# Lower weight halves from a negating ScalarE copy and an adding DMA

## Chip, core and metric

The kernel runs on one core of a Trainium2 chip. The core has TensorE (PE: matrix multiplications, and PEld: the loads of their stationary operand), VectorE (DVE), ScalarE (ACT), GpSimd (POOL) and SyncE (SP), which issues DMAs. Each engine works through its own queue in order; semaphores order work between engines. 16 DMA engines move data between DRAM, the on-chip memory SBUF, and back. TensorE writes its sums into eight banks of PSUM. The metric is the device time of one execution in microseconds (us), as the median of several runs.

## The reference

The reference is one inference step of a decoder with two layers and a width of 1024, for 512 prompt tokens and 64 sample tokens (8 sequences of 8) that share all weights. The first layer mixes tokens by a pooling mixer, the second by a gated delta-rule mixer (GDN) with a short convolution and a recurrent state; after each mixer stands a SwiGLU feed-forward block (FFN) of width 2816. All is float32. Most of the work is in products with weights:

```python
def swiglu(h, w_in, w_out):
    gu = h @ w_in
    return (jax.nn.silu(gu[..., :D_FF]) * gu[..., D_FF:]) @ w_out
...
    # gdn_mixer
    proj = h @ w_in
    qkv = proj[..., :GDN_CONV_DIM]
    z = proj[..., GDN_CONV_DIM:GDN_CONV_DIM + GDN_V_DIM]
...
    y = o.reshape(B, L, GDN_V_DIM).astype(h.dtype) @ w_out
```

Between these stand norms, the convolution, the chunked delta rule (triangular solves, a scan over chunks of 64 tokens) and the gate. Returned are the outputs of both groups and their new pooling, convolution and recurrent states.

## The kernel before

**Products in three passes.** The products are made in the format float32r (F32R in the code), to which a copy of a float32 tile is rounded. Each float32 operand w is kept as two F32R tiles: the upper half h = round(w) and the lower half l = w - h. A product is the sum of three matrix products, wh by ah, wh by al and wl by ah, all into one PSUM bank. The function `mm3` (lines 663 to 669) writes them in turn for each of up to 8 blocks of 128 rows, so the first product with wl comes right after the first two with wh:

```python
            PE.matmul(ps, wh[:, k], ah, start=first and k == 0, stop=False)
            PE.matmul(ps, wh[:, k], al, start=False, stop=False)
            PE.matmul(ps, wl[:, k], ah, start=False, stop=last and k == nk - 1)
```

**Weight tiles.** A weight tile is 1024 rows by 128 columns (896 rows in 48 of the loads of `ffn_w_out`), laid out as 128 partitions by 8 blocks by 128 columns: 512 KB, which in DRAM are 1024 runs of 512 bytes. `Weights.load` (line 650) takes a buffer `wraw`, lets SyncE issue the DMA, and calls `split` (line 655): ScalarE copies `wraw` into `wh`, which rounds; then VectorE subtracts, `wl = wraw - wh`. The subtraction may go to GpSimd instead (`EITHER`), where the planner finds that better. `wraw`, `wh` and `wl` have three buffers each (`Weights(ctx, 3, 3)`, line 838); a buffer can be filled again when the instructions that use its earlier content are done. There are 257 calls of `load` (one of them for a tile of only 32 columns); two more tiles, those of the pooling mixer (`load_pw`, line 923), call `split` directly after their own DMAs.

**Token halves.** The 576 tokens are worked on as two halves of 256 and 320 tokens (`HALVES`), which use PSUM banks "A" and "B". In the FFN (`ffn`, line 759) the weights are walked in 68 chunks: gate and up columns of a block of 7 or 8 slices of the hidden width, then the eight output columns of that block. In the middle of the walk one loaded tile serves both halves. At the beginning (14 chunks in the first layer, 10 in the second) and at the end (the last 8 chunks) the first half runs through all these chunks, and then the second half, and each half loads the weights anew:

```python
            for half in range(2):
                for i in range(lo, hi):
                    run(i, half, load(i))
```

The GDN output projection does the same for its second 1024 rows (line 1707). The GDN input projections, in four groups of heads, use each tile for both halves and lie between the delta-rule work of the groups.

**Order of the work.** The kernel doesn't issue its instructions as it writes them. The class `Plan` records them with their dependencies (data, and reuse of buffers) and simulates the five engines with a cost for each instruction (`cost`, line 143): how long it holds its engine and when its result is there. `forward` (line 339) places instructions on engines by priority; `finish` (line 250) repeats that with changed priorities 40 times and issues the best order found, engine by engine. For a DMA the model holds SyncE 60 ns, and lets transfers follow one another at 240 bytes per ns (`forward`, lines 468 to 470). In the model VectorE and GpSimd exclude each other for some instructions (lines 460 to 465). Where TensorE would be idle the planner puts matrix products of no use (`ps_w`). Nearly every instruction is thus issued from one line of `finish`, line 283, so profile rows are told apart by tile names.

Of the kernel before, what the change touches and what calls it, by code (L numbers as in the profile page):

```python
# [12 lines left out]
F32R = mybir.dt.float32r  # L13
I32 = mybir.dt.int32
AF = mybir.ActivationFunctionType
ALU = mybir.AluOpType
# [4 lines left out]
P = 128  # L21
# [29 lines left out]
class Plan:  # L51
# [91 lines left out]
    def cost(self, eng, method, out, ins, k):  # L143

        n = self.size(out)
        if method == "dma_start":
            return 60.0, 2000.0 + n * list(out.ap)[0][1] * 4 / 240.0
        ps = any(x.space == PSUM for x in ins)
        if eng == "PE":
            rows = self.rows(ins[0])  # L150
            if ins[0].dtype != F32:
                t = 0.4375 * n + 6.5
            elif method == "transpose":
                t = max(n / 1.2 + 2, 62.0)
            else:
                t = 2 * (n / 1.2 + 4.5)
                if rows == 128:
                    t = max(t, 220.0) if "tile_position" not in k else max(t / min(3.2, 128 / list(out.ap)[0][1]), 80.0)
                elif k.get("tile_position"):
                    t = t * 0.55 if rows == 64 else 62.0  # L160
            return t, t + 165
        if eng == "ACT":
            extra = 93 * sum(self.is_ap(k.get(w)) for w in ("scale", "bias")) + (100 if "accum_out" in k else 0)
            t = 0.833 * max(n, 16) + (170 if ps else 205) + extra
            return t - 102, t
        if eng == "POOL":
            if method in ("memset", "tensor_copy"):
                t = 0.85 * n + (100 if method == "memset" else 183)
            elif method == "affine_select":
                t = 1.1 * n + 190  # L170
            else:
                bc = any(list(x.ap)[-1][0] == 0 for x in ins if self.size(x) > 1)
                t = (1.75 if bc else 2.2) * n + 180
            return t - 60, t
        if method == "transpose":
            flat = all(list(x.ap)[-1][0] == 1 for x in ins + [out])
            t = 1.27 * n + 50 if flat else 1.95 * n + 80
        elif method == "scalar_tensor_tensor":
            t = 1.04 * n + 210
        elif method == "reciprocal":  # L180
            t = 6.2 * n + 153
        elif method in ("tensor_copy", "tensor_scalar") and not ps:
            t = 0.58 * n + 160
        else:
            t = 1.04 * n + 160
        return t - 85, t
# [152 lines left out]
    def forward(self, rank):  # L339
        ops, succ = self.ops, self.succ  # L340
        n = len(ops)
# [5 lines left out]
        mode, dma = {}, 0.0  # L347
# [10 lines left out]
        def note(t, work):  # L358
            nonlocal busy, fast
            for p in phases:  # L360
                while int((t + p[0]) / self.WINDOW) > p[3]:
                    p[1:] = 0.0, 1.0 if p[1] >= self.LOAD * self.WINDOW else 2.0, p[3] + 1
                p[1] += work
            fast = sum(p[2] for p in phases) / 4
            busy += work
            recent.append((t, work))
            while recent and recent[0][0] <= t - self.WINDOW:
                busy -= recent.popleft()[1]
# [36 lines left out]
        while todo:  # L405
            best = None
            for e in free:
                q, r = avail[e], ready[e]
                while q and taken[q[0][1]]:
                    heapq.heappop(q)  # L410
                while r and taken[r[0][1]]:
                    heapq.heappop(r)
                if q:
                    t = free[e]
                elif r:
                    t = max(free[e], r[0][0])
                else:
                    continue
                if best is None or t < best[0]:
                    best = t, e  # L420
            t, e = best
            if e == "PE" and t > free[e] + 300.0:
                idle_until(t)
            while ready[e] and ready[e][0][0] <= t:
                _, i = heapq.heappop(ready[e])
                if not taken[i]:
                    heapq.heappush(avail[e], (-rank[i], i))
            q = mine = avail[e]
            if e == "POOL":

                spare = sum(ops[y[1]][1]["DVE"][0] for y in avail["DVE"] if not ops[y[1]][8] and not taken[y[1]])
                spare += max(free["DVE"] - max(t, port["DVE"]), 0.0)
                mine = [x for x in q if not taken[x[1]] and ("DVE" not in ops[x[1]][0] or
                        spare > self.SPARE * ops[x[1]][1][e][0])]
                if not mine:
                    soon = [r[0][0] for r in (ready[e], ready["DVE"]) if r and r[0][0] > t]
                    if free["DVE"] > t:
                        soon.append(free["DVE"])
                    free[e] = max(t + 50.0, min(soon, default=t))
                    continue  # L440
            elif e == "DVE" and port["POOL"] > t + 300:
                mine = [x for x in q if not taken[x[1]] and not ops[x[1]][8]] or q
            i = self.take(e, mine, taken, mode.get(e))
            if mine is not q:
                q.remove((-rank[i], i))
                heapq.heapify(q)
            hold, done = ops[i][1][e]
            m = ops[i][5]
            if m and m != mode.get(e):
                if e in mode:  # L450
                    change = self.TURN[e][abs(m - mode[e]) > 500]
                    hold, done = hold + change, done + change
                mode[e] = m
            if e == "PE":
                note(t, ops[i][6])
                done += hold * (fast - 1)
                hold *= fast
            taken[i] = True
            todo -= 1
            if e == "DVE" and ops[i][8] or e == "POOL" and ops[i][9] != "memset":  # L460
                other = port["POOL" if e == "DVE" else "DVE"]
                late = max(other - 130.0 - t, 0.0)
                hold, done = hold + late, done + late
                if e == "DVE" or ops[i][9] == "tensor_tensor":
                    port[e] = t + done
            free[e] = t + hold
            end = t + done
            if e == "SP":
                dma = max(dma, t + 1400) + (done - 2000)
                end = dma + 600  # L470
            order.append((i, e))
            times.append((t, end))
            for name in ops[i][10]:
                still[name] -= 1
                quiet[name] = max(quiet.get(name, 0.0), end)
            for j in succ[i]:
                at = t + hold if ops[j][7] == e == "PE" else end + self.LAT[ops[j][7]]
                when[j] = max(when[j], at)
                left[j] -= 1
                if not left[j]:  # L480
                    arrive(j)
# [17 lines left out]
def hybrid_kernel(  # L499
# [11 lines left out]
    PE, ACT, DVE, POOL, SP = (plan.engine(**{name: real}) for name, real in (  # L511
        ("PE", nc.tensor), ("ACT", nc.scalar), ("DVE", nc.vector), ("POOL", nc.gpsimd), ("SP", nc.sync)))
# [68 lines left out]
    nk = sp.tile([P, SP1, KH], F32, name="nk")  # L581
# [63 lines left out]
    class Weights:  # L645
# [3 lines left out]

        def load(self, src, row, col, nk, n=P, eng=EITHER):  # L650
            raw = self.p.tile([P, 8, P], F32, name="wraw", tag="wraw", bufs=self.raw)[:, :nk, :n]
            SP.dma_start(raw, src[row:row + nk * P, col:col + n].rearrange("(k p) m -> p k m", p=P))
            return self.split(raw, eng)

        def split(self, raw, eng=EITHER):
            _, nk, n = raw.shape
            h = self.p.tile([P, 8, P], F32R, name="wh", tag="wh", bufs=self.bufs)[:, :nk, :n]
            l = self.p.tile([P, 8, P], F32R, name="wl", tag="wl", bufs=self.bufs)[:, :nk, :n]
            ACT.activation(h, raw, AF.Copy)
            eng.tensor_tensor(l, raw, h.bitcast(F32), op=sub)  # L660
            return h, l
# [177 lines left out]
    with ExitStack() as s0:  # L839
        xp = pool("xp0", stack=s0)  # L840
        x = xp.tile([P, NC, T], F32, name="x")
        y = {o0: xp.tile([P, NC, n], F32, name="y%d" % o0) for o0, n in HALVES}
        tp = pool("tp0", stack=s0)
        with ExitStack() as st:
# [12 lines left out]
            for g0, src in ((G_MPRE, norm_mix_pre), (G_MPOST, norm_mix_post), (G_FPRE, norm_ffn_pre),  # L857
                            (G_FPOST, norm_ffn_post), (G_PS, pool_scale)):
                n = src.shape[0] * NC
# [72 lines left out]
            for hi, (o0, n) in enumerate(HALVES):  # L932
                tag = "AB"[hi]
# [25 lines left out]
                for gi, g in enumerate((3, 2, 1, 0)):  # L959
# [20 lines left out]
                    wh, wl = pw[g // 2 * 2]  # L980
# [716 lines left out]
    x = xp.tile([P, NC, T], F32, name="x1")  # L1697
# [105 lines left out]
```

## Time and profile before

| | |
|---|---|
| time, median of 2 runs | 1650.04 us (1646.67 to 1653.41) |
| span of the profiled execution | 1654.1 us (the page gives no time outside the span) |
| busy TensorE (PE) | 1620.4 us, 98% |
| busy VectorE / ScalarE / GpSimd | 1002.7 / 699.4 / 119.5 us |
| mean granted TensorE clock | 0.989 |
| DMA | 185.25 MB, mean 112 GB/s |
| read from DRAM, written to it | 157.73 MB, 25.77 MB |

How to read it: a row names the line, the engine, the operation, the tile written and, after the arrow, the tiles read. Groups end with the busy time, the mean of one instruction in ns, and the idle time of the engine just before them with what ended most of it. `ps_A`, `ps_B`, `ps_m` and the like are PSUM banks, so rows of PE go by the bank and the operands. PE's matmuls are pipelined: one row of 309 ns overlaps the next. The chain of waits is followed back from the last instruction. In the table by stretches each engine has its busy time and, in brackets, the count of its instructions; then follow the granted clock (1.00 is full), the mean busy share of the 16 DMA engines and what they moved. The DMA engines' share can come out a little above 1 in a window of one microsecond.

### The profile page before, as it was taken

How to read it: one execution, taken by the hardware profiler on the slowest of the kernel's cores; microseconds unless marked ns; L12 is line 12 of the kernel's file. 1: busy time of each engine (PE TensorE's matmuls, PEld its weight loads, DVE VectorE, ACT ScalarE, POOL GpSimd, SP SyncE). 2: the span in 40 equal slices, each digit the busy share in tenths (PEclk: the TensorE clock that was granted, in tenths of full speed). 3: DMA queues.
4: the chain of work that ended last, by engine and by line, in shares of the span. 5: the costliest groups of instructions: out<-in, count | busy, mean ns of one | idle time of the engine just before them, and what ended most of it. 6: DMA issues, size and time to landing. Idle time of an engine off the chain costs nothing. (4 is left out here: it accounts for less than half of the span.)

```text
span 1654.1 us, 30525 instructions
## 1 busy us (share of the span) xinstructions
PE 1620.4 (98%) x12317; PEld 1567.2 (95%) x12317; DVE 1002.7 (61%) x2074; ACT 699.4 (42%) x1434; POOL 119.5 (7%) x265
## 2 busy tenths in 40 slices
PE   8999999999999999999999999999999999999997
PEld 8999999999999998998898899899999999999997
DVE  6784223333387798997998899656694312233244
ACT  6653233212365944553453554424464322222244
POOL 3010000000001010021121131100000000000000
PEclk8899999999999999999999999999999999999999
DMA  6255322223366233324323423557544323223333
GB/s 175 67 157 146 90 77 81 86 77 90 92 171 167 84 104 93 100 75 137 89 77 104 116 78 116 163 167 244 171 135 135 102 75 92 72 79 92 87 102 113
DMA packets 329812, 185.25 MB, mean 112 GB/s; under 512 B 12235, under 2 KB 324140, under 8 KB 329407
## 3 DMA queue, kind: packets, MB, share of 16 engines
q1 hardware_dynamic: 329671, 183.30, 38.2%
q8 instruction: 97, 1.59, 0.4%
q14 instruction: 44, 0.36, 0.1%
HBM read 157.73 MB, written 25.77 MB: 111 GB/s over the span
## 5 line engine op out<-in xcount | busy, mean ns | idle before, releaser
L283 DVE TENSOR_TENSOR wl<-wraw,wh 128x1024 fp32r<-128x1024 f32 (+2 forms) x253 | 301.9, 1201 | 292.1 <-PE ps_A L283 102.6
L283 ACT ACTIVATE wh<-wraw 128x1024 fp32r<-128x1024 f32 (+2 forms) x259 | 266.4, 1035 | 481.5 <-PE ps_A L283 185.9
L283 PE MATMUL ps_m<-hH,wh 128*128 128x256 f32 (+1 forms) x832 | 239.1, 309 | 1.4 <-ACT zz L283 1.2
L283 PE MATMUL ps_m<-hL,wh 128*128 128x256 f32 (+1 forms) x832 | 238.9, 308 | 0.0
L283 PE MATMUL ps_m<-hH,wl 128*128 128x320 f32 (+1 forms) x832 | 236.7, 309 | 0.0
L283 PE MATMUL ps_B<-hL,wh 128*128 128x320 f32 x768 | 224.2, 311 | 0.3 <-DVE hL L283 0.3
L283 PE MATMUL ps_B<-hH,wl 128*128 128x320 f32 x768 | 223.9, 311 | 0.1
L283 PE MATMUL ps_B<-hH,wh 128*128 128x320 f32 x768 | 223.3, 311 | 0.3 <-ACT sg L283 0.3
L283 PE MATMUL ps_A<-hH,wh 128*128 128x256 f32 x768 | 205.6, 285 | 1.3 <-DVE yo L283 1.3
L283 PE MATMUL ps_A<-hL,wh 128*128 128x256 f32 x768 | 204.1, 284 | 0.0
L283 PE MATMUL ps_A<-hH,wl 128*128 128x256 f32 x768 | 202.7, 284 | 0.1
L283 PEld LDWEIGHTS ps_m<-hH,wh 128*128 128x128 f32 x832 | 152.5, 190 | 6.5 <-ACT zz L283 1.8
L283 PEld LDWEIGHTS ps_m<-hL,wh 128*128 128x128 f32 x832 | 152.5, 190 | 2.2 <-DVE hL L283 0.2
L283 PEld LDWEIGHTS ps_m<-hH,wl 128*128 128x128 f32 x832 | 151.8, 190 | 2.8 <-issue 0.9
L283 PEld LDWEIGHTS ps_A<-hH,wh 128*128 128x128 f32 x768 | 142.8, 191 | 2.3 <-issue 1.4
L283 PEld LDWEIGHTS ps_A<-hL,wh 128*128 128x128 f32 x768 | 142.7, 191 | 0.2
L283 PEld LDWEIGHTS ps_A<-hH,wl 128*128 128x128 f32 x768 | 141.8, 191 | 0.4 <-DVE wl L283 0.2
L283 PEld LDWEIGHTS ps_B<-hL,wh 128*128 128x128 f32 x768 | 141.2, 189 | 0.6 <-DVE hL L283 0.5
L283 PEld LDWEIGHTS ps_B<-hH,wl 128*128 128x128 f32 x768 | 141.2, 189 | 0.5 <-DVE wl L283 0.2
L283 PEld LDWEIGHTS ps_B<-hH,wh 128*128 128x128 f32 x768 | 140.4, 189 | 0.9 <-ACT sg L283 0.5
L283 PE MATMUL ps_B<-aH,wh 128*128 128x320 f32 x352 | 102.1, 311 | 0.0
L283 PE MATMUL ps_B<-aL,wh 128*128 128x320 f32 x352 | 102.0, 310 | 0.0
(388 smaller groups left out, 3109.1 us busy)
## 6 DMA issues: line engine op xcount, KB each, us to landing
wraw<-in_ffn_w_in_dram SPq DMA_DIRECT2D x112, 512.0 KB
wraw<-in_gdn_w_in_dram SPq DMA_DIRECT2D x56, 512.0 KB
wraw<-in_ffn_w_out_dram SPq DMA_DIRECT2D x48, 448.0 KB
wraw<-in_gdn_w_out_dram SPq DMA_DIRECT2D x24, 512.0 KB
wraw<-in_ffn_w_out_dram SPq DMA_DIRECT2D x16, 512.0 KB
St<-in_state_gdn_rec_dram SPq DMA_DIRECT2D x32, 256.0 KB
out_dram<-St SPq DMA_DIRECT2D x32, 256.0 KB
z_d<-zz SPq DMA_DIRECT2D x16, 288.0 KB
```

The source lines that it names most:

```text
L283: calls[e](*a, **k)
```

## The change

`Weights.load` no longer calls `split`. After the load of `wraw` ScalarE first writes the negated upper half into the tile of the lower half, `l = -round(wraw)` (a copy with scale -1.0 into an F32R tile). GpSimd then issues a DMA that reads the same weights from DRAM a second time and adds them to that tile, `l += w`. Last ScalarE writes `h = round(wraw)` as before. `wl` now depends on ScalarE and on two DMAs, and no longer on VectorE or on `wh`. The two pooling tiles keep `split`. The planner's model is told of the new instruction: a DMA issued from GpSimd holds that engine 1000 ns, takes twice the transfer time of one from SyncE in the common DMA stream, and is left out of the exclusion between VectorE and GpSimd.

```diff
         if method == "dma_start":
-            return 60.0, 2000.0 + n * list(out.ap)[0][1] * 4 / 240.0
+            return 60.0 if eng == "SP" else 1000.0, 2000.0 + n * list(out.ap)[0][1] * 4 / 240.0
...
-            if e == "DVE" and ops[i][8] or e == "POOL" and ops[i][9] != "memset":
+            if e == "DVE" and ops[i][8] or e == "POOL" and ops[i][9] not in ("memset", "dma_start"):
...
-            if e == "SP":
-                dma = max(dma, t + 1400) + (done - 2000)
+            if ops[i][9] == "dma_start":
+                dma = max(dma, t + 1400) + (done - 2000) * (1 if e == "SP" else 2)
                 end = dma + 600
...
         def load(self, src, row, col, nk, n=P, eng=EITHER):
             raw = self.p.tile([P, 8, P], F32, name="wraw", tag="wraw", bufs=self.raw)[:, :nk, :n]
-            SP.dma_start(raw, src[row:row + nk * P, col:col + n].rearrange("(k p) m -> p k m", p=P))
-            return self.split(raw, eng)
+            w = src[row:row + nk * P, col:col + n].rearrange("(k p) m -> p k m", p=P)
+            SP.dma_start(raw, w)
+            h, l = self.tiles(nk, n)
+            ACT.activation(l, raw, AF.Copy, scale=-1.0)
+            POOL.dma_start(l, w, accum_op=ALU.add)
+            ACT.activation(h, raw, AF.Copy)
+            return h, l
+
+        def tiles(self, nk, n):
+            return tuple(self.p.tile([P, 8, P], F32R, name=x, tag=x, bufs=self.bufs)[:, :nk, :n] for x in ("wh", "wl"))
 
         def split(self, raw, eng=EITHER):
             _, nk, n = raw.shape
-            h = self.p.tile([P, 8, P], F32R, name="wh", tag="wh", bufs=self.bufs)[:, :nk, :n]
-            l = self.p.tile([P, 8, P], F32R, name="wl", tag="wl", bufs=self.bufs)[:, :nk, :n]
+            h, l = self.tiles(nk, n)
             ACT.activation(h, raw, AF.Copy)
             eng.tensor_tensor(l, raw, h.bitcast(F32), op=sub)
             return h, l
```

## Prediction

> **What bounds the kernel now.** I read the page from the top: the span, the busy table, the chain of waits by line, the costliest groups.
>
> ```profile
> span 1654.1 us, 30525 instructions
> ...
> PE 1620.4 (98%) x12317; PEld 1567.2 (95%) x12317; DVE 1002.7 (61%) x2074; ACT 699.4 (42%) x1434; POOL 119.5 (7%) x265
> ...
> PE ps_B L283 16%; PE ps_A L283 13%; PE ps_m L283 4%; PE ps_s L283 1%; PE ps_k L283 1%; PE ps_n L283 1%; DVE ac L283 1%; DMA yo<-y_d 0%; PE ps_w L279 0%; PE ps_x L283 0%; DVE wl L283 0%; DVE ii L283 0%; ACT wh L283 0%; DVE xT L283 0%; DMA og<-og_d 0%
> ...
> L283 DVE TENSOR_TENSOR wl<-wraw,wh 128x1024 fp32r<-128x1024 f32 (+2 forms) x253 | 301.9, 1201 | 292.1 <-PE ps_A L283 102.6
> L283 ACT ACTIVATE wh<-wraw 128x1024 fp32r<-128x1024 f32 (+2 forms) x259 | 266.4, 1035 | 481.5 <-PE ps_A L283 185.9
> ```
>
> TensorE is busy 98% of the span and idle for 1654.1 - 1620.4 = 33.7 us. The subtraction that the change removes costs VectorE 301.9 us, but in the chain of waits "DVE wl" has 0%. So VectorE is relieved where nothing waits for it, and the most that any relief can give is those 33.7 us, 2.0% of the span. A measurement of this kernel can tell about 2% (33 us) from no change.
>
> The average hides two kinds of stretches, so I read the busy table by stretches. The first table is of the whole kernel; the second, of the same stretches, is of the instructions that touch wl alone. There DVE (x) plus POOL (x) counts the weight tiles that are split.
>
> ```profile
> core 0: us, PE busy (x) PEld busy (x) DVE busy (x) ACT busy (x) POOL busy (x), PEclk, DMA share, GB/s
> 59.00:108.00 49.00, 49.00 (x383) 48.32 (x383) 40.21 (x89) 27.99 (x50) 4.41 (x5) 0.95 0.48 139
> 108.00:155.00 47.00, 46.67 (x315) 46.09 (x316) 25.54 (x38) 20.62 (x32) 0.00 (x0) 1.00 0.48 140
> 155.00:430.00 275.00, 275.00 (x2067) 274.92 (x2066) 80.73 (x114) 73.99 (x115) 0.00 (x0) 1.00 0.29 84
> 430.00:485.00 55.00, 54.88 (x419) 54.45 (x418) 36.68 (x70) 28.32 (x49) 2.45 (x3) 1.00 0.49 139
> 485.00:540.00 55.00, 54.31 (x410) 51.75 (x409) 42.18 (x84) 29.20 (x54) 4.23 (x10) 1.00 0.66 173
> 540.00:1000.00 460.00, 446.95 (x3508) 414.43 (x3507) 415.55 (x977) 241.51 (x587) 71.45 (x146) 0.99 0.34 96
> 1000.00:1140.00 140.00, 136.81 (x1124) 129.76 (x1125) 101.82 (x225) 56.94 (x147) 11.03 (x16) 1.00 0.52 158
> 1140.00:1200.00 60.00, 58.66 (x455) 58.16 (x454) 38.12 (x73) 23.66 (x41) 3.85 (x4) 1.00 0.67 210
> 1200.00:1270.00 70.00, 69.68 (x524) 68.22 (x523) 53.37 (x111) 39.83 (x69) 3.54 (x3) 1.00 0.47 136
> 1270.00:1590.00 320.00, 320.00 (x2402) 319.69 (x2401) 95.42 (x140) 85.04 (x138) 0.00 (x0) 1.00 0.30 87
> 1590.00:1654.00 64.00, 55.69 (x414) 52.88 (x412) 34.05 (x58) 32.18 (x60) 0.00 (x0) 0.97 0.38 118
> ```
>
> ```profile
> core 0: us, PE busy (x) PEld busy (x) DVE busy (x) POOL busy (x), PEclk, DMA share, GB/s
> 59.00:108.00 49.00, 31.27 (x116) 22.23 (x116) 17.27 (x14) 0.00 (x0) 0.95 0.48 139
> 108.00:155.00 47.00, 29.21 (x102) 18.63 (x103) 14.59 (x12) 0.00 (x0) 1.00 0.48 140
> 155.00:430.00 275.00, 165.26 (x689) 118.48 (x689) 53.12 (x45) 0.00 (x0) 1.00 0.29 84
> 430.00:485.00 55.00, 34.64 (x135) 23.77 (x134) 18.17 (x17) 0.00 (x0) 1.00 0.49 139
> 485.00:540.00 55.00, 32.75 (x123) 21.15 (x122) 15.99 (x14) 0.00 (x0) 1.00 0.66 173
> 540.00:1000.00 460.00, 172.51 (x602) 110.12 (x602) 45.59 (x36) 12.62 (x5) 0.99 0.34 96
> 1000.00:1140.00 140.00, 60.38 (x217) 39.26 (x217) 14.62 (x12) 2.39 (x1) 1.00 0.52 158
> 1140.00:1200.00 60.00, 29.62 (x112) 19.98 (x111) 16.77 (x14) 0.00 (x0) 1.00 0.67 210
> 1200.00:1270.00 70.00, 41.22 (x153) 27.28 (x152) 23.26 (x20) 0.00 (x0) 1.00 0.47 136
> 1270.00:1590.00 320.00, 191.03 (x801) 137.18 (x801) 62.59 (x53) 0.00 (x0) 1.00 0.30 87
> 1590.00:1654.00 64.00, 30.53 (x113) 20.24 (x112) 15.06 (x14) 0.00 (x0) 0.97 0.38 118
> ```
>
> In 155:430 and 1270:1590 a weight tile serves both token halves and is used up in 275/45 = 6.1 us. In 59:155, 430:540, 1140:1270 and 1590:1654 it mostly serves one half only: 49/14 = 3.5 us, 55/17 = 3.2 us. These **tight stretches** already hold the DMA engines at 0.47 to 0.67. They decide the result.
>
> **The change part by part.** *VectorE loses* the 257 subtractions of the table, some 300 us. Only where VectorE is nearly full can that help: 540:1000 (415.55 of 460 us busy), where TensorE idles 13 us, and 1000:1140, where it idles 3 us. About a tenth of VectorE's work there goes (45.59 of 415.55). I take 5 us off; the bounds are 0 and 16.
>
> *ScalarE gains* a second pass over each weight tile: 257 x 1035 ns = 266 us, so 699 becomes 965 us, 58% of the span. The fullest stretch is 59:108: 27.99 + 14 x 1.04 = 42.5 of 49 us. It still fits, so I cost it at nothing, with little cover: if that stretch gets no longer, PSUM reads and the weight passes queue behind each other on ScalarE. The new pass waits for the buffer's last reader on TensorE, as wh does now (185.9 us for ps_A in its row above), and the second pass and all PSUM copies are queued behind it. The planner orders them by modelled times.
>
> *GpSimd gains* 257 DMA issues, *the DMA engines* a second read of every weight. No row here shows a DMA issued by GpSimd or one that adds, so both prices are bounds. One plain 512 KB load, alone on the engines in three neighbouring microseconds, and the two issue-like rows:
>
> ```profile
> 280.00:281.00 1.00, 1.00 (x10) 1.00 (x9) 0.66 (x2) 0.28 (x1) 0.00 (x0) 1.00 0.30 86
> 281.00:282.00 1.00, 1.00 (x10) 1.00 (x9) 0.00 (x0) 0.00 (x0) 0.00 (x0) 1.00 1.03 307
> 282.00:283.00 1.00, 1.00 (x10) 1.00 (x9) 0.00 (x0) 0.00 (x0) 0.00 (x0) 1.00 0.44 131
> ...
> 279.53 0.37 SPq L283 DMA_DIRECT2D wraw<-in_ffn_w_in_dram  x1
> ...
> L283 POOL TENSOR_TENSOR wl<-wraw,wh x6: 2387/2411/2980, 594.4 to 1026.6; 128x1024 fp32r<-128x1024 f32 x6
> ```
>
> The load takes 0.30 + 1.03 + 0.44 = 1.77 us of all 16 engines for 86 + 307 + 131 = 524 KB, in runs of 512 bytes (128 float32 columns of a weight row). An adding transfer moves the same runs, but must also read the old tile out of SBUF. Its lower bound is the plain price, 1.77 us; its upper bound I put at four plain transfers, 7.08 us (two reads, an add and a write that don't overlap). I take twice the plain price, 3.54 us, because two streams are read for one written, and the plain load, which overlaps its one read and one write, is the nearest row.
>
> By the Trainium skill, "DMA: Bandwidth & Descriptors", section "SDMA does more than copy", the adder reduces two streams elementwise; no row here shows it, and it agrees with the factor of two, not with the plain price.
>
> Now the sum. DMA time that a stretch needs = its share x its length + tiles x 3.54 us; what exceeds the length is lost, because TensorE can't multiply by weights that haven't landed:
>
> - 59:108: 0.48 x 49 + 14 x 3.54 = 73.1, loses 24.1
> - 108:155: 22.6 + 42.5 = 65.0, loses 18.0
> - 430:485: 27.0 + 60.2 = 87.1, loses 32.1
> - 485:540: 36.3 + 49.6 = 85.9, loses 30.9
> - 1140:1200: 40.2 + 49.6 = 89.8, loses 29.8
> - 1200:1270: 32.9 + 70.8 = 103.7, loses 33.7
> - 1590:1654: 24.3 + 49.6 = 73.9, loses 9.9
> - 155:430: 79.8 + 159.3 = 239 of 275; 540:1000: 302 of 460; 1000:1140: 119 of 140; 1270:1590: 284 of 320: nothing lost.
>
> Together 178.5 us. The two tiles that are ready in the buffers when a stretch begins save 2 x 3.54 = 7 us in each of four runs of tight stretches (59, 430, 1140, 1590), 28 us. Against that, each switch waits once for the longer chain of load, negation, issue and add, about 7 us (below). I let the two cancel.
>
> *The ring of three buffers* (wh and wl have three each). From the release of a buffer to the landing of its wl: 1.04 us of ScalarE, the issue, about 1 us to the first byte (the issue at 279.53 shows traffic from about 280.7), 3.54 us, some landing time. With 0.37 us (SyncE's issue row) as the lower bound of an issue and 2.41 us (GpSimd over 1024 elements per partition) as a middle value, that is 6.5 to 8.5 us. TensorE covers it with two tiles: 7 us in the tight stretches, 12.2 us in the paired ones. So the ring costs at most (3.5 + 8.5)/3 = 4.0 us per tile, less than the 1.77 + 3.54 = 5.3 us that the engines need anyway. Cost nothing beside the DMA's.
>
> *GpSimd's queue*: in 540:1140 it also holds 156 other instructions (162 less the 6 on wl; 67 us busy of 600), and an add that waits for its negation holds them back. It has 54 adds there; at 2.41 us each that is 130 us more, which fits. Nothing taken, at most some 20 us.
>
> *The planner* (its order is fixed before the run) books 1 us of GpSimd per add and twice the transfer time of a load, so every queue is ordered anew. I cost the new order at nothing. The bounds are a gain of 33.7 us (all of TensorE's idle time) and a loss of the same size.
>
> Sum: 1654.1 + 178.5 - 5 = 1827.6 us for an execution like the profiled one. Its span is 0.25% above the median of the runs (1650.04; the page shows no time outside the span): 1827.6 x 1650.04/1654.1 = 1823, **forecast 1825 us**, own range 1750 to 1950.
>
> **The rivals.**
>
> *The cover holds (not slower).* An adding transfer costs the engines no more than a plain one. The same sums with 1.77 us lose 2.1 + 6.1 + 5.0 = 13.2 us (430:540 and 1140:1200 only), less 5: 1662, scaled 1658 us. It decides below about 2.05 us per add, where the losses reach 33 us. For it: the paired stretches, at a share of 0.29 and 0.30, have room for any price up to 4 us. Against it: every tight stretch is then at 0.94 to 1.1 of the engines, with no room for order. By the Trainium skill, "DMA: Bandwidth & Descriptors", section "Anatomy of one DMA", a transfer issued by GpSimd takes about 2.0 us plus its bytes at 436 GB/s, an estimate of 1.2 us of movement here; by that the cover would hold. The trace disagrees for these 512-byte runs: 524 KB in 1.77 us is 296 GB/s.
>
> *GpSimd becomes the bound.* The issue isn't one instruction's work but 1024 runs' work. If GpSimd writes for each run two reads and one write, each at its elementwise price (2411/1024 = 2.35 ns), an add holds it 7.23 us. Then each stretch needs tiles x 7.23 us: 101, 87, 325, 123, 101, 297, 94, 101, 145, 383 and 101 us in the order of the table, and the excesses 52 + 40 + 50 + 68 + 46 + 41 + 75 + 63 + 37 = 472 us give 2121 us. It decides from about 5.3 us per issue. For it: it is the only work that scales with runs on one engine. Against it: SyncE issues the same 1024 runs in 0.37 us, and nothing shows that GpSimd needs more.
>
> *The adder is the slow part.* At 7.08 us per add all stretches but 540:1000 lose: 74 + 61 + 123 + 92 + 80 + 25 + 79 + 104 + 151 + 59 = 848 us, about 2497 us.
>
> *It pays.* VectorE's relief fills TensorE's idle time: at most 33.7 us, 1620 us, which also needs the cover to hold.
>
> **How the numbers follow.** Forecast 0.42, GpSimd the bound 0.24, slow adder 0.14, cover holds 0.18, it pays 0.02. The range is 1665 to 2330: it takes in the forecast's case, GpSimd's with issues up to about 8 us, and the upper part of the cover's; the slow adder and the ends beyond, about 2 in 10, are left out. Faster by over 2%: 0.02. Within 2%: 0.12, two thirds of the cover's case. Slower: 0.86.
>
> **What would show it.** Right: the losses sit in the tight stretches, with a DMA share near 1 there, while 155:430 and 1270:1590 keep their length; a new queue of GpSimd carries some 130 MB and takes a share of about twice the weights' present one; PE waits for DMA wl. Wrong: if the paired stretches grow too and the DMA share stays well below 1, GpSimd (solid with issues) or the latency of the ring is the bound; if the adds' packets take more than twice the plain ones, the adder is; if no stretch grows, the cover held; if the granted clock, 0.95 in 59:108 and 1.00 elsewhere in the tight stretches, falls in the gaps, the loss grows by TensorE's slower work. VectorE must lose some 300 us and ScalarE gain some 266 us in every case.

## The result, and the profile after

The changed kernel takes 1937.85 us (median of 2 runs, 1937.03 to 1938.66) against 1650.04 us: 1.175 times as long, 95% interval 1.169 to 1.180. That is 288 us more.

The page of the changed kernel: span, busy time, DMA queues, the chain of waits by line, and the groups that touch the weight tiles, with the group of idle products (`ps_w`).

```profile
span 1935.2 us, 34530 instructions
...
PE 1842.7 (95%) x14079; PEld 1765.6 (91%) x14079; DVE 746.1 (39%) x1852; ACT 920.5 (48%) x1690; POOL 493.0 (25%) x487
...
q0 software_dynamic: 261136, 131.22, 55.0%
q1 hardware_dynamic: 329671, 183.30, 33.4%
...
PE ps_B L283 9%; PE ps_A L283 8%; DMA wl<-in_ffn_w_out_dram 1%; POOL wl L283 0%; ACT wl L283 0%; DVE xT L283 0%; PE ps_w L279 0%; DVE yo L283 0%; ACT wh L283 0%; ACT nh L283 0%; ACT nsq L283 0%; PE ps_n L283 0%; DVEq L1806 0%; ACT aH L283 0%; ACT sg L283 0%
...
L283 POOL DMA_DIRECT2D wl<-in_ffn_w_in_dram x112 | 174.1, 1555 | 526.4 <-ACT sg L283 194.1
L283 ACT ACTIVATE wl<-wraw 128x1024 fp32r<-128x1024 f32 (+1 forms) x257 | 262.5, 1022 | 3.8 <-DMA wraw<-in_gdn_w_out_dram 2.7
L279 PE MATMUL ps_w<-ones 128*128 128x128 f32 x1966 | 258.0, 276 | 1.3 <-POOL ones L88 1.3
...
wl<-in_ffn_w_in_dram POOLq DMA_DIRECT2D x112, 512.0 KB, 7.2
```

VectorE did lose its work (1002.7 to 746.1 us) and ScalarE gained 262.5 us. The new queue q0 carries 131 MB and holds the 16 engines for 0.55 x 1935.2 = 1064 us, 4.14 us for each of 257 adds in the mean. In the kernels below with the same adds in other orders or in fewer places it is 4.1 to 4.2 us as well. TensorE looks nearly as busy as before, 95% against 98%, but 258.0 us of that are products of no use, 1966 of them (204 before): the planner foresaw the gaps and filled them, so they don't show as waits.

The table by stretches of the changed kernel, cut where the same pieces of work begin, under it the negations alone, whose count is that of the weight tiles (there the columns are ScalarE's busy time and count, the clock, the DMA share and GB/s), and last the idle products alone in the four tight stretches (PE and PEld).

```profile
core 0: us, PE busy (x) PEld busy (x) DVE busy (x) ACT busy (x) POOL busy (x), PEclk, DMA share, GB/s
57.00:240.00 183.00, 166.94 (x1257) 160.98 (x1256) 38.98 (x102) 80.59 (x116) 50.77 (x35) 0.99 0.98 170
240.00:505.00 265.00, 264.66 (x1991) 264.47 (x1990) 28.90 (x70) 105.02 (x154) 66.57 (x42) 1.00 0.95 164
505.00:655.00 150.00, 139.25 (x1089) 133.99 (x1088) 48.67 (x116) 72.20 (x117) 48.00 (x37) 1.00 1.03 182
655.00:1280.00 625.00, 604.62 (x4774) 557.21 (x4773) 473.82 (x1172) 344.23 (x780) 139.93 (x187) 1.00 0.76 154
1280.00:1520.00 240.00, 216.80 (x1653) 207.89 (x1651) 61.47 (x160) 106.81 (x164) 59.50 (x41) 0.99 0.98 181
1520.00:1850.00 330.00, 328.19 (x2468) 327.03 (x2467) 36.54 (x88) 131.94 (x196) 84.46 (x53) 1.00 0.94 163
1850.00:1935.00 85.00, 71.23 (x530) 66.68 (x530) 18.99 (x39) 36.80 (x62) 20.78 (x12) 0.95 0.84 151
```

```profile
57.00:240.00 183.00, 31.26 (x30) 0.99 0.98 170
...
505.00:655.00 150.00, 25.40 (x27) 1.00 1.03 182
...
1280.00:1520.00 240.00, 36.37 (x35) 0.99 0.98 181
1520.00:1850.00 330.00, 54.23 (x54) 1.00 0.94 163
```

```profile
57.00:240.00 183.00, 58.68 (x452) 55.56 (x452) 0.99 0.98 170
...
505.00:655.00 150.00, 52.46 (x406) 49.31 (x406) 1.00 1.03 182
...
1280.00:1520.00 240.00, 89.06 (x706) 85.20 (x706) 0.99 0.98 181
...
1850.00:1935.00 85.00, 24.64 (x182) 22.80 (x182) 0.95 0.84 151
```

The four tight stretches were 96, 110, 130 and 64 us long before; now they are 183, 150, 240 and 85 us, 258 us more (the boundaries are good to some 10 us). Of the idle products, 224.8 us lie there. The DMA share is 0.98 to 1.03 there, except in the last. A tile takes 183/30 = 6.1 us there. The paired stretches went from 275 and 320 to 265 and 330 us at a share of 0.94 to 0.95: hardly touched. The GDN stretch went from 600 to 625.

### The profile page after: what moved, and what is told of

Same layout as the page of the kernel before. It is cut to its first block, busy times and chain, and to the rows that moved or that the text cites. A ratio compares the mean times of both kernels' runs of the same rounds, so it can differ in the third digit from the quotient of the medians.

```text
span 1935.2 us, 34530 instructions
## 1 busy us (share of the span) xinstructions
PE 1842.7 (95%) x14079; PEld 1765.6 (91%) x14079; DVE 746.1 (39%) x1852; ACT 920.5 (48%) x1690; POOL 493.0 (25%) x487
## 5 line engine op out<-in xcount | busy, mean ns | idle before, releaser
L283 POOL DMA_DIRECT2D wl<-in_ffn_w_in_dram x112 | 174.1, 1555 | 526.4 <-ACT sg L283 194.1
L283 ACT ACTIVATE wl<-wraw 128x1024 fp32r<-128x1024 f32 (+1 forms) x257 | 262.5, 1022 | 3.8 <-DMA wraw<-in_gdn_w_out_dram 2.7
L279 PE MATMUL ps_w<-ones 128*128 128x128 f32 x1966 | 258.0, 276 | 1.3 <-POOL ones L88 1.3
L283 PE MATMUL ps_B<-hH,wh 128*128 128x320 f32 x768 | 242.3, 315 | 17.8 <-ACT wh L283 9.2
L283 PE MATMUL ps_m<-hH,wh 128*128 128x320 f32 (+1 forms) x832 | 244.6, 312 | 1.5 <-ACT wh L283 0.7
L279 PEld LDWEIGHTS ps_w<-ones 128*128 128x128 f32 x1966 | 242.6, 192 | 2.5 <-POOL ones L88 1.3
L283 PE MATMUL ps_B<-hH,wl 128*128 128x320 f32 x768 | 241.8, 315 | 0.0
L283 PE MATMUL ps_m<-hL,wh 128*128 128x320 f32 (+1 forms) x832 | 239.0, 304 | 0.0
L283 DVE TENSOR_TENSOR sg<-sg,ps_B 128x320 f32<-128x320 f32 x44 | 21.4, 486 | 433.4 <-PE ps_B L283 413.2
L283 POOL DMA_DIRECT2D wl<-in_ffn_w_out_dram x64 | 107.7, 1684 | 262.2 <-ACT wl L283 95.1
```

The costliest lines, as they stand in the source:

```text
L279: self.tc.nc.tensor.matmul(self.banks[i[0]][i[1]][0][:, :self.idle.shape[1]], self.idle, self.idle, start=True, stop=True)
L283: calls[e](*a, **k)
```

## The experiments

**Theory after the result**: the adds fill the DMA engines in the tight stretches. Rivals: ScalarE's second pass; the chain behind a buffer (negation, issue, landing); anything that GpSimd issues is slow; the planned order with its idle products.

### ScalarE's pass alone

```diff
-            POOL.dma_start(l, w, accum_op=ALU.add)
             ACT.activation(h, raw, AF.Copy)
+            eng.tensor_tensor(l, raw, l.bitcast(F32), op=add)
```

> Keeps the second ScalarE pass (l = -round(w)) and replaces the adding DMA by an addition on VectorE (l = w + l); nothing of the computation is left out. Theory 'full DMA engines' (the adds fill the DMA engines in the stretches that use a weight tile for one token half): the DMA share goes back to 0.3 to 0.6 and the time to 1645 to 1665 us. Rival 'ScalarE' (the extra 266 us of passes, in one queue with the PSUM copies): a good part of the 288 us stays, over 1720 us.

1659.5 us against 1654.72 us of the kernel before, run beside it, ratio 1.003 (1.001 to 1.005). ScalarE's extra pass, in an order planned for it, costs 5 us: small, but not nothing. The other 283 us come with the DMA.

### Adds in the loose stretches only, and in the tight ones only

```diff
-        def load(self, src, row, col, nk, n=P, eng=EITHER):
+        def load(self, src, row, col, nk, n=P, eng=EITHER, again=True):
...
             SP.dma_start(raw, w)
+            if not again:
+                return self.split(raw, eng)
```

The first kernel passes `again=False` in the FFN's head and tail, the early GDN projections of the first half, and the second half of the GDN output projection; the second passes it everywhere else. By the adds in the traces these are 153 and 104 tiles; the expectations counted 161 and 96.

> The adding DMA only for the 161 tiles that are not in the one-half stretches (FFN middle, GDN projections, first half of the GDN output projection); the other 96 are split by VectorE as before. Full DMA engines: a paired tile needs 1.77 us (load) + 4.14 us (add: 55.0% of 1935.2 us by 257) = 5.9 us against 6.1 us of TensorE, so nearly nothing is lost: 1650 to 1680 us. Rival 'chain' (the 7.2 us from issue to landing, behind the negation, stalls the ring of three buffers wherever it is used): the paired stretches grow too, over 1720 us.

> The mirror of the kernel with adds in the loose stretches only: the adding DMA only for the 96 tiles that serve one token half; all others are split by VectorE. If the one-half stretches hold the loss, nearly all of the 283 us stays, less the 21 us that the loose tiles cost alone: 1900 to 1935 us. If the loss comes from the number of adds wherever they are, 96/257 of it: about 1760 us.

Loose only: 1676.18 us against 1654.72, ratio 1.015 (1.009 to 1.020). Tight only: 1918.94 against 1649.35, ratio 1.163 (1.161 to 1.165). The losses, 21 and 270 us, add up to that of the whole change. So the place is shown: 104 of the 257 adds make 270 of 288 us. In the loose kernel the paired stretch of the first layer stands at a DMA share of 0.96, and in its old length TensorE does nearly as many products as before (2064 against 2067). Under it the GDN stretch:

```profile
155.00:430.00 275.00, 274.58 (x2064) 274.38 (x2063) 29.64 (x71) 108.73 (x159) 68.62 (x44) 1.00 0.96 166
540.00:1140.00 600.00, 578.48 (x4573) 532.54 (x4572) 465.98 (x1166) 332.67 (x761) 135.79 (x182) 1.00 0.76 153
```

There TensorE does less than before in the same 600 us (578.48 us busy, 583.77 before), though VectorE is relieved.

### Adds in the GDN stage only

As the loose kernel, and the middle of the FFN is split as before, too:

```diff
-                    w = load(i)
+                    w = load(i, again=False)
```

57 adds are left (the expectation said 65).

> The adding DMA only in the GDN stage (64 projection and gate tiles less the eight that serve the first half alone, and the eight of the first half of the output projection: 65), where VectorE is nearly full; all FFN tiles are split by VectorE as before. This asks what VectorE's relief is worth where the DMA engines have room. The prediction took 5 us off (bounds 0 and 16): 1640 to 1650 us against 1650. If the relief is worth nothing, or the adds disturb GpSimd's queue and ScalarE there: 1650 to 1665 us.

1673.11 against 1651.48 us, ratio 1.014 (1.012 to 1.016): longer than both expectations. Whatever VectorE's relief gains where VectorE is fullest, the adds cost 22 us more there. The loose tiles cost 21 us in all, so the paired stretches cost about nothing and the GDN stage all of it. The traces agree: from the first to the last product on `ps_m` (the GDN projections) it is 606 us before, 632 us with the loose adds and 634 us with these. Which wait makes these 22 us was not settled.

### What the add costs: no reading of the old tile, no add at all

```diff
-            POOL.dma_start(l, w, accum_op=ALU.add)
+            POOL.dma_start(l, w)
```

> As the changed kernel, in the same planned order, but the DMA from GpSimd doesn't add: it overwrites l by w, rounded to float32r (so l is not the lower half: the addition is left out of the computation). The old tile isn't read. 'Two streams': its 512-byte packets fall from 66 ns to 27 to 35 ns and queue q0 from 55% to under 30%. Rival 'software queue' (what GpSimd issues is slow whatever it does): still 60 to 70 ns. Time: if the idle products that the planner put into TensorE's queue (1966, some 250 us) are what sets the pace, it stays over 1850 us although the engines are relieved; if the DMA engines set it, it falls below 1750 us.

The second kernel is the one before, with the weight loads moved to GpSimd; the planner books such a load at the plain transfer time. Against the changed kernel:

```diff
-                dma = max(dma, t + 1400) + (done - 2000) * (1 if e == "SP" else 2)
+                dma = max(dma, t + 1400) + (done - 2000)
...
-            SP.dma_start(raw, w)
-            h, l = self.tiles(nk, n)
-            ACT.activation(l, raw, AF.Copy, scale=-1.0)
-            POOL.dma_start(l, w, accum_op=ALU.add)
-            ACT.activation(h, raw, AF.Copy)
-            return h, l
+            POOL.dma_start(raw, w)
+            return self.split(raw, eng)
```

> The kernel before (VectorE subtracts) with the 257 weight loads issued by GpSimd instead of SyncE: plain DMAs, no second read. Two streams: 512-byte packets of q0 take 27 to 32 ns as those of q1 did (28.7 ns), GpSimd is held about 1.55 us per issue, and the time is 1645 to 1680 us. Rival 'software queue': 60 ns and more per packet, a DMA share near 1 in the one-half stretches, over 1700 us.

The queue, the issue group and the landing of the overwriting kernel, then of the kernel with plain loads from GpSimd:

```profile
q0 software_dynamic: 261136, 131.22, 44.1%
...
L283 POOL DMA_DIRECT2D wl<-in_ffn_w_in_dram x112 | 98.3, 877 | 594.4 <-ACT wl L283 444.4
...
wl<-in_ffn_w_in_dram POOLq DMA_DIRECT2D x112, 512.0 KB, 5.6
```

```profile
q0 software_dynamic: 36144, 131.22, 27.6%
...
L283 POOL DMA_DIRECT2D wraw<-in_ffn_w_in_dram x112 | 99.2, 886 | 449.2 <-DVE wl L283 363.3
...
wraw<-in_ffn_w_in_dram POOLq DMA_DIRECT2D x112, 512.0 KB, 4.8
```

Plain loads from GpSimd cost 0.276 x 1654.3/257 = 1.78 us of the engines each, the price of SyncE's, and the kernel takes 1656.0 us. The software queue isn't slow by itself; that rival falls. GpSimd is held 0.89 us per issue; 1.55 had been expected. By the Trainium skill, "DMA: Bandwidth & Descriptors", section "Issuing engines are not separate DMA queues", DMAs of all issuers run on the same 16 engines; the price of 1.78 against 1.77 us agrees.

The overwriting kernel missed both expectations of its price; its time is the one expected if the planned idle products set the pace. It takes 0.441 x 1914.8/257 = 3.29 us per tile, in records that take 52 ns for 512 bytes in the mean, between 28.7 ns (SyncE's before) and 66 ns (the adds). So of the 2.37 us that an add costs above a plain load, 1.52 us come already with a DMA that rounds to float32r, and 0.85 us with the add and its reading. And its time, 1916.66 us, hardly fell although a fifth of the adds' DMA time was gone. Then the engines can't be all that sets the pace. (This kernel, the one with GpSimd's loads and those with long runs were run once each, so differences of some 10 us say little.)

### The same bytes in long runs

```diff
-            POOL.dma_start(l, w, accum_op=ALU.add)
+            POOL.dma_start(l, src[0:P, 0:nk * n].rearrange("p (k m) -> p k m", k=nk), accum_op=ALU.add)
```

> As the changed kernel, in the same order, but each add reads 128 rows of 1024 neighbouring columns (runs of 4 KB) instead of 1024 runs of 512 bytes: as many bytes of other weights, so the computation of the lower halves is left out. If the add's price goes by runs, queue q0 falls from 55% of the engines to under 40%; if by bytes, it stays at 50% and more. GpSimd's 1.55 us per issue falls below 1.0 us if it goes by runs. Time 1900 to 1940 us, since the planned idle products stay.

```profile
q0 software_dynamic: 37904, 131.22, 38.3%
...
L283 POOL DMA_DIRECT2D wl<-in_ffn_w_in_dram x112 | 96.9, 865 | 599.8 <-ACT wl L283 494.8
```

An add in runs of 4 KB takes 0.383 x 1924.8/257 = 2.87 us of the engines and holds GpSimd 0.87 us instead of 1.56. All adds from one weight tensor then read the same rows, so the length of a run and the place in DRAM changed together. Time 1926.55 us, again nearly unmoved in the same order.

### The planner's prices and its idle products

```diff
-                dma = max(dma, t + 1400) + (done - 2000) * (1 if e == "SP" else 2)
+                dma = max(dma, t + 1400) + (done - 2000) * (0.81 if e == "SP" else 1.9)
```

> The changed kernel with the planner's prices set to the measured ones: a load 1.77 us of transfer (was 2.18), an add 4.15 us (was 4.37), a GpSimd issue 1.55 us (was 1.00). Only the order and the number of idle products change. 'DMA engines set the pace': 5.9 us per tile either way, so 1920 to 1945 us. 'The plan sets it' (6.55 us per tile were booked, and the gaps filled with idle products that TensorE must work off): the sum of the prediction with 4.14 us per add, 1885 to 1910 us.

with 1550 ns instead of 1000 for GpSimd's hold. The next kernel keeps the prices of the change, and returns at once from the function that fills TensorE's gaps:

```diff
         def idle_until(t):
 
-            at = free["PE"]
-            t -= max(300.0, self.LEAVE * (t - at))
+            return
```

> The changed kernel without idle products in planned gaps of TensorE; prices as in the change. TensorE then waits at semaphores instead. DMA engines set the pace: 1920 to 1950 us, longer if the granted clock falls. The plan's idle products set it: 1885 to 1910 us, with TensorE's waits for DMA wl of 150 us and more in the table of waits.

1894.91 us (ratio 1.150, 1.146 to 1.153) and 1884.57 us (1.142, 1.140 to 1.144). So these two orders win back 43 and 53 of the 288 us: the change books 2.18 + 4.37 = 6.55 us of transfer per tile, the records take 1.77 + 4.14 = 5.9, and with the measured prices the idle products fall from 1966 to 1506. Rows of the kernel without idle products:

```profile
57.00:225.00 168.00, 124.28 (x767) 116.82 (x767) 39.25 (x104) 78.25 (x114) 48.95 (x34) 0.89 1.06 183
225.00:500.00 275.00, 274.42 (x2061) 273.75 (x2060) 31.32 (x72) 110.65 (x160) 69.86 (x44) 1.00 0.94 163
500.00:640.00 140.00, 108.57 (x689) 99.10 (x687) 46.91 (x112) 73.39 (x117) 50.03 (x40) 0.90 1.13 199
...
1250.00:1470.00 220.00, 162.83 (x1047) 151.06 (x1046) 73.55 (x183) 112.58 (x184) 58.54 (x40) 0.90 1.11 208
```

TensorE's gaps are now visible (124 of 168 us busy), the granted clock falls to 0.89, and the DMA share rises to 1.06 to 1.13 in the tight stretches. A share is the sum of the records' times over 16 engines, and it passes 1 in stretches of over 100 us too, so 1 doesn't mean that the engines can do no more. The expected waits for DMA wl of 150 us weren't there. The longest in the table of TensorE's waits are for `wh`, ScalarE's last pass over a tile:

```profile
PE ps_B L283 <- ACT wh L283: 25.1, 28, 2.1
PE ps_A L283 <- ACT wh L283: 22.1, 25, 4.1
```

Why TensorE comes to wait for that pass was not settled; the order may place it late, since by its prices `wl` is later still.

### Cheaper adds without idle products

The edits of the long runs and of the overwriting DMA, each together with the early return of `idle_until`.

> The long runs (wrong weights are added, so the lower halves are not computed) without idle products. An add takes 2.87 us of the DMA engines there (38.3% of 1924.8 us by 257). The sum of the prediction by stretches with 2.87 us loses 108 us: 1750 to 1765 us, if the DMA engines set the pace. If the chain behind them does (negation, issue, 7 us to landing, the late wh pass on ScalarE), it stays over 1820 us.

> The rounding DMA that overwrites (the addition is left out, so the lower halves are not computed) without idle products. It takes 3.29 us of the DMA engines (44.1% of 1914.8 us by 257); the sum by stretches loses 152 us: 1790 to 1810 us if the DMA engines set the pace, over 1850 us if the chain does.

1869.1 and 1846.33 us, where 1750 to 1765 and 1790 to 1810 had been expected if the engines set the pace, and over 1820 and over 1850 if the chain does. The dearer of the two adds gives the shorter time. Rows of the kernel with long runs:

```profile
57.00:225.00 168.00, 126.83 (x792) 119.67 (x792) 39.38 (x106) 81.29 (x119) 29.44 (x35) 0.90 0.84 185
...
500.00:640.00 140.00, 109.42 (x713) 101.02 (x712) 47.01 (x115) 74.96 (x122) 31.22 (x42) 0.91 0.92 203
...
1250.00:1470.00 220.00, 161.22 (x1027) 150.31 (x1025) 70.34 (x177) 112.76 (x179) 35.06 (x41) 0.88 0.89 208
```

The DMA share is lower (0.84 to 0.92), yet TensorE's busy time is nearly that of the kernel with dear adds. So the price of an add on the engines does not set this pace. What is left of the suspects is the fixed order (it still books 6.55 us per tile, and each engine's queue waits in that order) and the chain behind a buffer; the times of these two runs don't tell them apart.

### A planner that trusts the transfers

```diff
-                dma = max(dma, t + 1400) + (done - 2000) * (1 if e == "SP" else 2)
+                dma = max(dma, t + 1400) + (done - 2000) * 0.81
```

Load and add are thus booked at 1.77 us alike (GpSimd's hold at 1550 ns).

> The changed kernel, adds and all, with a planner that books an add at the plain price: 1.77 us of transfer each for load and add, 3.54 us per tile, against 5.9 us that the engines really take (the change books 6.55, 'plan_measured' 5.92). Nothing else differs. 'The engines are the floor': below their real price a lower booking gains nothing, and the sum of the prediction with 4.14 us per add holds: 1875 to 1900 us. 'The booked order is what costs' (long runs and the overwriting DMA, without idle products, still took 1869 and 1846 us): the time falls on with the booking, below 1850 us. If orders that trust too much in the transfers stall elsewhere: above 1910 us.

1975.86 us, ratio 1.197 (1.193 to 1.202): the worst of all. Its table by stretches and TensorE's waits:

```profile
1520.00:1850.00 330.00, 285.94 (x1973) 281.93 (x1973) 30.45 (x72) 106.16 (x156) 67.50 (x43) 0.93 0.77 131
```

```profile
PE ps_B L283 <- DMA wl<-in_ffn_w_in_dram: 58.1, 42, 4.9
PE ps_B L283 <- DMA wl<-in_ffn_w_out_dram: 35.3, 21, 4.0
```

Now even a paired stretch loses time, at a DMA share of only 0.77: TensorE stands before tiles whose add has not landed. So the time from issue to landing (8.1 us in the median for `ffn_w_in`) does stall the kernel where the order doesn't allow for it.

In the first tight stretch, though, this kernel is the faster one:

```profile
100.00:150.00 50.00, 40.60 (x278) 37.97 (x278) 16.66 (x45) 28.61 (x43) 17.97 (x13) 0.97 1.29 226
150.00:200.00 50.00, 40.98 (x260) 38.88 (x259) 4.90 (x10) 23.46 (x30) 15.97 (x11) 0.97 1.25 222
```

21 tiles are negated in these 100 us, 4.8 us per tile, with the same adds. The engines move 222 to 226 GB/s, against 170 in the first tight stretch of the changed kernel. So its share of 0.98 there was not the engines' limit.

### Who waits for whom: landing and first product

The traces hold the landing of each add and TensorE's first product with the tile's `wl`. The n-th add belongs to the n-th tile that TensorE uses; in no kernel of the table does a tight tile's first product come before its landing. The table takes the 104 tiles of the tight stretches (for the pace, tiles 6 to 28 of the first one).

| kernel | us per tile | landing to first product, median | started within 0.1 us of landing |
|---|---|---|---|
| the change | 6.09 | 5.5 us | 5 of 104 |
| measured prices | 5.66 | 3.8 us | 6 of 104 |
| no idle products | 5.46 | 1.7 us | 29 of 104 |
| long runs, no idle products | 5.44 | 1.9 us | 17 of 104 |
| overwriting, no idle products | 5.19 | 3.1 us | 5 of 104 |
| hopeful prices | 4.73 | 0.04 us | 67 of 104 |

In the changed kernel nearly every add has landed long before TensorE comes to its tile. There TensorE waits neither for the DMA engines nor for the chain: it works through its queue, in the planned order and with the planned idle products. So the theory that the adds fill the engines falls for this kernel. Without idle products, too, most tiles have landed before TensorE starts them (75, 87 and 99 of 104), so there it is mostly the order. In the first tight stretch of the hopeful plan (tiles 6 to 28) it starts 20 of 23 tiles as they land, and a tile's negation starts 0.9 us after the last product with the buffer's former tile. There the ring of three buffers is the bound: from that last product to the landing it takes 10.4 us. How much of this is transfer and how much latency was not separated.

An estimate from this pace: the 105 tiles that the prediction counts in 400 us of tight stretches would take 105 x 4.73 = 497 us, some 100 of the 258 us that these stretches grew by. The rest would be the order; but no order was found that has this pace there and loses nothing elsewhere.

## Why the prediction was right or wrong

**Right: sign, place and range.** 1937.85 us lies in 1665 to 2330, and in the forecast's own range of 1750 to 1950. The loss sits in the tight stretches (270 of 288 us by the adds there alone), the paired ones keep their length, q0 carries 131 MB at over twice the old price, and neither VectorE's relief nor ScalarE's load moves the end much.

**Mis-sized: the add.** "I take twice the plain price, 3.54 us": it is 4.14 us. The upper bound of 7.08 us was too high, the reason given (two streams read for one written) not quite the right one: rounding into float32r alone makes 3.29 us. The sum by stretches with 4.14 us loses 241.5 us instead of 178.5 and gives 1654.1 + 241.5 - 5 = 1890.6 us, scaled 1886. The kernels whose order books the measured prices, or has no idle products, take 1894.91 and 1884.57. That is luck in good part, since the wait that the sum stands for is not the one that holds these kernels.

**Wrong: "I cost the new order at nothing."** Two other orders win back 43 and 53 us, and by the table of landings the order holds more than that. The prediction said that the planner books one load and two more per tile, but not that TensorE would then work through planned idle products instead of taking a tile when it lands. For the same reason "PE waits for DMA wl" was a poor sign: such waits are nearly absent from the page, and `ps_w` with 258.0 us stands in their place.

**Wrong: "what exceeds the length is lost, because TensorE can't multiply by weights that haven't landed".** In the changed kernel 99 of the 104 adds in the tight stretches had landed over 0.1 us before TensorE's first product with them, in the median 5.5 us before. What exceeds the length is lost there by plan: the planner makes much the same sum (loads and adds one after another, an add at twice a load) before the run, and lays TensorE's queue out by it. So the forecast is near for a reason that it did not give, and that is luck. Nor is a share of 1 the most that the engines do: in the hopeful plan it was 1.27 for 100 us. With adds of 2.87 and 3.29 us the same sum would give some 1753 and 1797 us, and 1869.1 and 1846.33 were measured. What the adds cost in the best order was not found.

**Partly wrong: the ring, "Cost nothing beside the DMA's".** I reckoned 6.5 to 8.5 us from release to landing. In the changed kernel it is 9.5 us in the median (tiles 6 to 28 of the first tight stretch): 0.9 us until the negation starts, 1.0 us for the negation, a gap of some 0.4 us, and 7.2 us from the start of the issue to the landing. That costs the changed kernel nothing, since its adds land early. In the hopeful plan the ring does bound the first tight stretch, at 4.73 us per tile, and this is less than the 1.77 + 4.14 = 5.9 us that the sum would give the engines. A ring of four was not run.

**Wrong in sign, small: VectorE's relief.** I took 5 us off; adds in the GDN stage alone cost 22 us.

**Small misreadings.** The last tight stretch, 1590:1654, has a DMA share of 0.38 and a clock of 0.97, outside the "0.47 to 0.67" and the "1.00 elsewhere" of the prediction; with plain prices it would stand at 0.77, not at 0.94 or more. And a DMA share comes out above 1 not only in windows of one microsecond.

**Rivals.** *GpSimd the bound* falls: 1.56 us per issue, not 7.23, and it is busy 25% of the time. *The adder is the slow part* holds in direction only: 4.14 us, not 7.08. *The cover holds* falls by price: it needed an add under 2.05 us. With it falls the estimate by the Trainium skill, "DMA: Bandwidth & Descriptors", section "Anatomy of one DMA": 2.0 us plus 1.2 us of movement, 3.2 us in all; an adding DMA of 512 KB in 512-byte runs lands 7.2 us after its issue in this kernel, and a plain one from GpSimd 4.8 us.

## What to carry to other kernels

Before work is moved from an engine off the critical path to the DMA engines, cost the DMA in the stretch where its share is highest: a mean of 38% hid stretches at 0.5 to 0.67, where each weight tile is used once. Until it is measured, take a DMA that rounds at nearly twice and one that adds at over twice the price of a plain one (here 3.29 and 4.14 against 1.78 us). In a kernel whose order is computed from prices, a changed price is a change of its own: look for planned idle work as well as for waits, and try the corrected prices before the hardware is blamed. A high DMA share doesn't show that anybody waits for the DMA; compare the landing of a tile with its first use.

## What was unexpected of the hardware

Per weight tile (512 KB, 48 of 257 with 448 KB) in 512-byte runs the records of the DMA engines sum to 1.77 us for a plain load (SyncE, one tile), and in the mean to 1.78 us for a plain load (GpSimd), 3.29 us for a rounding DMA and 4.14 us for an adding DMA; in 4 KB runs, always of the same rows, an adding one took 2.87 us. For the tiles of `ffn_w_in` GpSimd was held about 0.88 us by the issue of a plain or rounding DMA, whose 1024 runs cost it no more than the 128 runs of the long adds (0.87 us), and 1.56 us by an adding DMA of 1024 runs. The mean busy share of the DMA engines, taken from their records, stood at 1.27 for 100 us with loads and adds together (224 GB/s), so a share of 1 is no ceiling.
